# The end of a hybrid decoder step, cut into two halves of its tokens

## The chip, the cores and the metric

The kernel runs on one NeuronCore of a Trainium2 chip. Its time is the device time of one execution in microseconds (us); the kernel before has a median of 1413.08 us over three runs (1413.05 to 1415.09). The engines of the core work in parallel, each on its own list of instructions, and wait for each other through semaphores: TensorE (PE in the profile, with PEld for its weight loads) multiplies matrices, VectorE (DVE) and GpSimd (POOL) do elementwise work, ScalarE (ACT) does elementwise functions, and SyncE (SP) issues most transfers. ScalarE issues some transfers too.

## The reference

One decoder layer is applied to 264 tokens (256 of a prompt and 8 single tokens of a decoding batch), with a model width of 2048 and everything in float32:

```python
xn = rms_norm(x, g_mix)
z = xn @ w_in                       # five slices, for three mixers
# pooling branch, RG-LRU branch, Conformer branch -> y_pool, y_lru, y_conf
gates = sigmoid(xn @ w_gate + b_gate)
x = x + (g_a * y_pool + g_b * y_lru + g_c * y_conf) @ w_out
hid = square(relu(rms_norm(x, g_mlp) @ w_up))
x = x + hid @ w_down
y = x * rsqrt(mean(x * x, axis=-1) + 1e-6) * g_final
```

The last line is where the change lies. It can start for good only when the last column block of `hid @ w_down` has been added, since the mean goes over all 2048 features. The kernel also returns the new states of the three mixers.

## The kernel before

Activations are stored with features on the 128 partitions and tokens along the free dimension. `X` holds the 2048 features as 16 tiles (`KD`) of 128 x 264. Weights stream from memory in chunks of 128 x 1024 through SyncE; ScalarE rounds each chunk to a high part (`whi`, line 147), VectorE forms the low part (`wlo`, line 148), and three matmuls with the high and low parts (lines 151 to 153) stand for one float32 product. A loop over the chunks (line 847) gives out all instructions in one written order. After the last chunk of a group of four output tiles, an evacuation function is called for each of the four; work that may be done later is put in a list by `later(n, fn)` and given out by `run_bg`, at the end of the loop's round. Each engine takes its own instructions in the order in which they were given out.

For the last group (`w_down`, q = 3, tiles 12 to 15) the evacuation `down_evac` adds the result to `X` on VectorE (line 762) and puts off a function `rest`: it squares the tile on ScalarE (line 734), has GpSimd add the square to a running sum `sq2` (line 736; not for tiles 14 and 15, which keep their own squares), and scales the tile in place by `gfin`, which is -0.5 times `g_final` (line 767). The last two chunks are multiplied tile by tile, so tile 12 is complete first and tile 15 last.

Then comes the tail (lines 907 to 944). Three matmuls with a matrix of 1/2048 add the running sum and the two squares over the partitions and spread the mean to all of them (line 909). `root_seed` takes a logarithm and an exponential on ScalarE for a first inverse root (lines 209 and 210), and VectorE improves it by one Newton step in three instructions (lines 928, 929 and 931), which leave the factor in PSUM (`last`). ScalarE copies it to `rstd` in SBUF (line 932), which is what GpSimd reads. VectorE scales tiles 0 to 11 in place in six pieces of 1, 2, 3, 3, 2 and 1 tiles (line 936), each followed by a transfer on SyncE's queue (line 937); GpSimd scales tiles 12 to 15 one by one (line 940), each followed by a transfer on ScalarE's queue (line 941). The output in memory is laid out as partition, tile, token.

Between the root and the Newton step, 50 matmuls of ten shapes go to a PSUM buffer `probe` that nothing reads (lines 912 to 926). Two ScalarE instructions make operands for them: a copy of `whi` to bfloat16 (line 889), six chunks before the end, and a zeroed `wlo` chunk (line 911).

Of the kernel before, what the change touches and what calls it, by code (L numbers as in the profile page):

```python
# [9 lines left out]
F32 = mybir.dt.float32  # L10
F32R = mybir.dt.float32r
AF = mybir.ActivationFunctionType
ALU = mybir.AluOpType
AX = mybir.AxisListType

P = 128
D = 2048
# [28 lines left out]
NHI = 4  # L46
# [31 lines left out]
def hybrid_step(ctx: ExitStack, tc: tile.TileContext, x_in, par_in, st_in, wall, y_out, st_out):  # L78
# [5 lines left out]
    def f(ap):  # L84
        return ap.bitcast(F32)
# [24 lines left out]
    def acc():  # L110
        return psum.tile([P, 512], F32, name="acc", tag="acc")
# [58 lines left out]
    def mark(q, flag):  # L170
        stage(q, "none", 0.0, [lambda: done.add(flag)], 0)
# [34 lines left out]
    def root_seed(dst, ps, scale, load=True):  # L206
        if load:
            nc.scalar.preload_act_table_set(LN_EXP)
        nc.scalar.activation(dst, ps, AF.Ln, bias=eps, scale=scale)
        nc.scalar.activation(dst, dst, AF.Exp, scale=-0.5)  # L210
# [153 lines left out]
        stage("lru", "dve", 1.25, [lambda: gather(RA)])  # L364

    def lru_conv_sample():
        tmp = Gf[:, 8 * N:8 * N + 256].rearrange("p (c b k) -> p c b k", c=8, b=8)
        xs = XC[:, :, TP:N]

        def products():  # L370
            wb = pv("w_lru_conv").rearrange("p (c k) -> p c k", c=8)[:, :, None, :].to_broadcast([P, 8, 8, 4])
            nc.gpsimd.tensor_tensor(tmp, st_lc, wb, op=ALU.mult)
            nc.gpsimd.tensor_copy(st[:, O_LC:O_LC + 24].rearrange("p (c k) -> p c k", c=8), el[:, :, TP:TP + 3])

        def sums():
            nc.vector.tensor_reduce(xs, tmp, op=ALU.add, axis=AX.X)
            nc.vector.tensor_tensor(xs, xs, pv("b_lru_conv")[:, :, None].to_broadcast([P, 8, 8]), op=ALU.add)

        stage("lru", "pool", 1.0, [products])
        stage("lru", "dve", 0.5, [sums])  # L380

    def stage_split(q, n, hi, lo, x, gap=1):

        stage(q, "act", 0.65, [lambda i=i: nc.scalar.copy(hi(i), x(i)) for i in range(n)])
        stage(q, "dve", 0.71, [lambda i=i: nc.vector.tensor_tensor(lo(i), x(i), f(hi(i)), op=ALU.subtract)
                               for i in range(n)], gap)

    def lo_two(t, at=8):
        return lambda c: t[:, at + 2 * c:at + 2 * c + 2, :]

    def hi_two(t):
        return lambda c: t[:, 2 * c:2 * c + 2, :]
# [76 lines left out]
        stage("lru", "pool", 1.5, [sample])  # L469

    def gel_evac(ct, ps):
        nc.vector.tensor_tensor(GEL[:, ct, :], ps[:, :N], rstd, op=ALU.mult)
        spend(dve=0.4)

# [284 lines left out]
        later(2 + m % 4 // 2, other)  # L759

    def down_evac(q, m, ps):
        nc.vector.tensor_tensor(X[:, m, :], X[:, m, :], ps[:, :N], op=ALU.add)
        spend(dve=0.4)
        if q == 3:
            def rest():
                square_add(m, m < KD - 2)
                nc.scalar.activation(X[:, m, :], X[:, m, :], AF.Copy, scale=gfin[:, m:m + 1])

            later(0 if m >= KD - 4 else 1 + m % 4 // 2, rest)
# [28 lines left out]
    def after(gi):  # L798

        name, _, _, m = groups[gi]  # L800
        if name == "w_in":
            if m == 2:
                lru_conv(range(4, 8))
                lru_conv_sample()
                stage_split("lru", 4, hi_two(L), lo_two(L), lambda c: XC[:, 2 * c:2 * c + 2, :])
                mark("lru", "xc")
            elif m == 5:
                conf()
            elif m == 0:
                pooling()  # L810
            elif m in (3, 4):
                if m == 4:
                    gelu(0)
                    gelu(2)
                    stage_split("lru", 4, lambda c: LH(two(c)), lambda c: LH(slice(8 + 2 * c, 10 + 2 * c)),
                                lambda c: GEL[:, two(c), :])
                    mark("lru", "lru")
# [7 lines left out]
    def tile_mm(i, c, kt, m, rhs, pss, stop):  # L825
        s = slice(kt * 512 + m * P, kt * 512 + (m + 1) * P)
        xh, xl = rhs(2 * c + kt)
        mm3(pss[m], whi[:, i % NHI, s], wlo[:, i % NHI, s], xh, xl, c == 0 and kt == 0, stop)

    bw = Gf[:, :1024].bitcast(mybir.dt.bfloat16)  # L830
    zw = wlo[:, (len(chunks) - 3) % NHI, :]


    x_tile(0)
# [12 lines left out]
    for i, ch in enumerate(chunks):  # L847
        now[0] = i
        split(i + AHEAD)
        if i == 12:  # L850
            softplus()
            nc.vector.tensor_scalar(gfin, pv("g_final"), -0.5, None, op0=ALU.mult)
        if i % 2 == 0:
            dma_pair((i + 8) // 2)
        if i == 2:
            nc.sync.dma_start(par, par_in)
            nc.sync.dma_start(st[:, :S_IN], st_in)
        if i < 5:
            x_tile(2 * i + 6)
            x_tile(2 * i + 7)  # L860
        kind, gi, c, _ = ch
        if kind == "dense":
            rhs, fn = group(gi)
            n = groups[gi][2] // 2
            if c == 0:
                pss = [acc() for _ in range(4)]
            if i < len(chunks) - 2:
                if i == 0:
                    first_mm(rhs, pss)
                for kt in range(i == 0, 2):  # L870
                    for m in range(4):
                        tile_mm(i, c, kt, m, rhs, pss, c == n - 1 and kt == 1)
            elif i == len(chunks) - 1:
                for m in range(4):
                    for b in range(4):
                        tile_mm(i - 1 + b // 2, c - 1 + b // 2, b % 2, m, rhs, pss, b == 3)
            if c == n - 1:
                for m in range(4):
                    fn(m, pss[m])
                after(gi)  # L880
        elif kind == "lru":
            for j in range(2):
                lru_gate_mm(2 * gi + j, i, j)
            if gi == 3:
                lru_tail()
        elif kind == "grp":
            grp_mm(i)
        if i == len(chunks) - 6:
            nc.scalar.copy(bw, whi[:, 0:2, :].rearrange("p a n -> p (a n)"))
        if i == len(chunks) - 4:  # L890
            nc.scalar.preload_act_table_set(LN_EXP)
        if i == 140:
            nc.gpsimd.dma_start(st_out, st)
        if 5 <= i < 9:
            x_squares(i - 5)
        if i == 9:
            later(0, x_sum)
        if i == 11:
            later(0, x_rms)
        run_bg()  # L900
# [3 lines left out]
    assert not any(queues.values())  # L904


    ps = acc()
    for k, t in enumerate((20, 21 + (KD - 2) % 3, 21 + (KD - 1) % 3)):
        nc.tensor.matmul(ps[:, :N], ones, G[:, t, :], start=k == 0, stop=k == 2)  # L909
    root_seed(rstd, ps[:, :N], 1.0, False)  # L910
    nc.scalar.activation(zw, f(whi[:, 0, :]), AF.Copy, scale=0.0)
    probe = acc()
    flat = A.rearrange("p a n -> p (a n)")
    for n, p, m, at, what in ((512, P, P, 0, "b"), (N, P, P, 0, "b"), (512, P, P, 0, "r"), (512, P, P, 4, "r"),
                              (256, P, P, 0, "r"), (320, P, P, 0, "r"), (N, P, 64, 0, "r"), (N, 64, P, 0, "r"),
                              (N, P, P, 0, "f"), (N, P, P, 0, "z")):
        for j in range(5):
            if what == "b":
                w, v = bw[:, 1024 + j * P:1024 + (j + 1) * P], bw[:, :n]
            elif what == "r":  # L920
                w, v = whi[:p, j % 4, j * P:j * P + m], flat[:p, at:at + n]
            elif what == "z":
                w, v = zw[:, j * P:(j + 1) * P], zw[:, :n]
            else:
                w, v = f(whi[:, j % 4, j * P:(j + 1) * P]), f(flat[:, :n])
            nc.tensor.matmul(probe[:m, :n], w, v, start=True, stop=True)  # L926
    t = G[:, 9, :]
    nc.vector.tensor_tensor(t, rstd, rstd, op=ALU.mult)
    nc.vector.scalar_tensor_tensor(t, ps[:, :N], EPS, t, op0=ALU.add, op1=ALU.mult)
    last = acc()  # L930
    nc.vector.scalar_tensor_tensor(last[:, :N], t, -3.0, rstd, op0=ALU.add, op1=ALU.mult)
    nc.scalar.copy(rstd, last[:, :N])
    at, own = 0, KD - 4
    for n in (1, 2, 3, 3, 2, 1):
        s = slice(at, at + n)
        nc.vector.tensor_tensor(X[:, s, :], X[:, s, :], last[:, None, :N].to_broadcast([P, n, N]), op=ALU.mult)
        nc.sync.dma_start(y_out[:, s, :], X[:, s, :])
        if at and own < KD:
            s = slice(own, own + 1)
            nc.gpsimd.tensor_tensor(X[:, s, :], X[:, s, :], rstd[:, None, :], op=ALU.mult)  # L940
            nc.scalar.dma_start(y_out[:, s, :], X[:, s, :])
            own += 1
        at += n
    assert (at, own) == (KD - 4, KD)

# [84 lines left out]
```

## Time and profile before

| what | value |
|---|---|
| median of three runs | 1413.08 us (1413.05 to 1415.09) |
| the profiled execution: its own time, its span | 1414.92 us, 1413.1 us |
| TensorE busy | 1406.7 us, 100% |
| VectorE, ScalarE, GpSimd busy | 830.0, 721.8, 98.1 us |
| data moved | 256.95 MB, mean 182 GB/s |
| the tail, from the last evacuation to the end of the span | 1399.57 to 1413.1 us |

The span runs from the first to the last instruction of the profiled execution; the time of a run is taken around it and is a little longer. Times in rows are microseconds from the start of the span. In rows of the timeline the columns are start, duration, engine, line, operation, output and inputs with their shape, and a count; in brackets stand the idle time before it and what ended it. In rows of groups the two numbers after the first bar are the busy time in all and the mean of one instruction in nanoseconds. In rows of stretches the engines' busy times are followed by the granted share of TensorE's clock, the busy share of the transfer engines and the rate in GB/s.

### The profile page before, as it was taken

The numbers are of one execution on the slowest core, as the hardware profiler recorded it, in microseconds if no ns is written. First come the engines' busy times: TensorE is split into PE (matmuls) and PEld (weight loads), VectorE is DVE, ScalarE is ACT, GpSimd is POOL, SyncE is SP. The second block draws the span as 40 slices with busy tenths as digits, with TensorE's granted clock in tenths as the row PEclk, the third lists the DMA queues.
The fourth block names the chain that finished last, engine by engine and source line by source line (L and its number), as shares of the span: only waits on it lengthen the run. The fifth ranks groups of instructions, "written<-read, shape, count | busy, mean of one in ns | idle before, by whom it ended". The sixth has DMA issues, their size and how long they took to land.

```text
span 1413.1 us, 26699 instructions
## 1 busy us (share of the span) xinstructions
PE 1406.7 (100%) x11472; PEld 1402.5 (99%) x11473; DVE 830.0 (59%) x1031; ACT 721.8 (51%) x1007; POOL 98.1 (7%) x122
## 2 busy tenths in 40 slices
PE   9999999999999999999999999999999999999999
PEld 8999999999999999999999999999999999999998
DVE  6685787776766648665545444544455544455443
ACT  6657577656564645454544334543344533354544
POOL 0230010110102103010000000000000000000012
PEclk9999999999999999999999999999999999999999
DMA  9455455555655554555555555555555555555551
GB/s 331 150 184 195 167 195 193 179 179 180 209 179 179 179 179 150 209 179 179 180 179 180 182 179 180 182 180 183 181 183 183 183 181 183 180 179 179 179 179 62
DMA packets 38998, 256.95 MB, mean 182 GB/s; under 512 B 4320, under 2 KB 5472, under 8 KB 9440
## 3 DMA queue, kind: packets, MB, share of 16 engines
q1 hardware_dynamic: 38160, 253.67, 52.5%
q8 instruction: 89, 1.46, 0.4%
q0 software_dynamic: 144, 1.04, 0.2%
q10 hardware_dynamic: 576, 0.54, 0.1%
q14 instruction: 29, 0.24, 0.0%
HBM read 252.03 MB, written 3.21 MB: 181 GB/s over the span
## 4 chain that ended last, share of the span: by engine, by line
PE 98%; DMA 1%; POOL 0%; DVE 0%; SPq 0%; ACT 0%; issue 0%; ACTq 0%
PE acc L153 33%; PE acc L151 32%; PE acc L152 32%; PE acc L926 1%; DMA GX<-x_dram 1%; POOL tmp L689 0%; POOL G L541 0%; POOL G L540 0%; SPq L134 0%; DVE wlo L148 0%; PE acc L547 0%; ACT whi L147 0%; PE acc L222 0%; SPq L138 0%; PE acc L909 0%
## 5 line engine op out<-in xcount | busy, mean ns | idle before, releaser
L148 DVE TENSOR_TENSOR wlo<-raw,whi 128x1024 fp32r<-128x1024 f32 (+1 forms) x480 | 586.4, 1223 | 555.0 <-ACT whi L147 553.3
L147 ACT CAST whi<-raw 128x1024 fp32r<-128x1024 f32 (+1 forms) x480 | 497.6, 1038 | 631.8 <-PE acc L152 580.0
L151 PE MATMUL acc<-A,whi 128*128 128x264 f32 x1980 | 565.4, 286 | 1.6 <-ACT A L230 1.6
L153 PE MATMUL acc<-A,wlo 128*128 128x264 f32 x1980 | 564.1, 285 | 0.2 <-DVE wlo L148 0.2
L152 PE MATMUL acc<-A,whi 128*128 128x264 f32 x1980 | 563.3, 284 | 0.2
L151 PEld LDWEIGHTS acc<-A,whi 128*128 128x128 f32 x1980 | 374.0, 189 | 2.0 <-ACT A L230 1.8
L152 PEld LDWEIGHTS acc<-A,whi 128*128 128x128 f32 x1980 | 374.9, 189 | 0.7 <-DVE A L231 0.6
L153 PEld LDWEIGHTS acc<-A,wlo 128*128 128x128 f32 x1980 | 374.2, 189 | 0.4 <-DVE wlo L148 0.4
L151 PE MATMUL acc<-xn,whi 128*128 128x264 f32 x1024 | 291.9, 285 | 0.0
L153 PE MATMUL acc<-xn,wlo 128*128 128x264 f32 x1024 | 291.3, 284 | 0.0
L152 PE MATMUL acc<-xn,whi 128*128 128x264 f32 x1024 | 290.8, 284 | 0.0
L152 PEld LDWEIGHTS acc<-xn,whi 128*128 128x128 f32 x1024 | 193.5, 189 | 0.0
L153 PEld LDWEIGHTS acc<-xn,wlo 128*128 128x128 f32 x1024 | 193.1, 189 | 0.0
L151 PEld LDWEIGHTS acc<-xn,whi 128*128 128x128 f32 x1024 | 193.0, 189 | 0.0
L152 PE MATMUL acc<-Q,whi 128*128 128x264 f32 x644 | 182.6, 284 | 0.0
L153 PE MATMUL acc<-LH,wlo 128*128 128x264 f32 x640 | 182.3, 285 | 0.0
L151 PE MATMUL acc<-LH,whi 128*128 128x264 f32 x640 | 182.0, 284 | 0.0
L152 PEld LDWEIGHTS acc<-Q,whi 128*128 128x128 f32 x644 | 121.5, 189 | 0.0
L153 PEld LDWEIGHTS acc<-LH,wlo 128*128 128x128 f32 x640 | 120.4, 188 | 0.0
L151 PEld LDWEIGHTS acc<-LH,whi 128*128 128x128 f32 x640 | 120.4, 188 | 0.0
L736 POOL TENSOR_TENSOR G<-G 128x264 f32<-128x264 f32 x28 | 25.7, 917 | 809.9 <-ACT G L734 808.9
L522 ACT ACTIVATE G<-tmp,par 128x256 f32<-128x256 f32 x120 | 54.3, 500 | 1.3 <-DVE G L536 0.7
(179 smaller groups left out, 781.3 us busy)
## 6 DMA issues: line engine op xcount, KB each, us to landing
raw<-wall_dram SPq DMA_DIRECT2D x230, 1024.0 KB, 4.9
raw<-wall_dram SPq DMA_DIRECT2D x11, 512.0 KB, 7.7
GX<-x_dram SPq DMA_DIRECT2D x7, 264.0 KB, 8.1
raw<-wall_dram SPq DMA_DIRECT2D x7, 256.0 KB, 3.4
so_dram<-st POOLq DMA_DIRECT2D x1, 1018.0 KB, 6.1
st<-st_dram SPq DMA_DIRECT2D x1, 912.0 KB, 8.3
y_dram<-GX SPq DMA_DIRECT2D x2, 396.0 KB, 3.3
y_dram<-GX ACTq DMA_DIRECT2D x4, 132.0 KB, 2.6
```

The costliest lines, as they stand in the source:

```text
L147: nc.scalar.copy(h[:, s], r[:, s])
L148: nc.vector.tensor_tensor(lo[:, s], r[:, s], f(h[:, s]), op=ALU.subtract)
L151: nc.tensor.matmul(ps[:, :N], whi_t, xh, start=first, stop=False)
L152: nc.tensor.matmul(ps[:, :N], whi_t, xl, start=False, stop=False)
L153: nc.tensor.matmul(ps[:, :N], wlo_t, xh, start=False, stop=last)
L522: nc.scalar.activation(dst[:, ct, :TP], vext[:, ct, k:k + TP], AF.Copy, scale=par[:, w:w + 1])
L736: nc.gpsimd.tensor_tensor(sq2, sq2, t, op=ALU.add)
L926: nc.tensor.matmul(probe[:m, :n], w, v, start=True, stop=True)
```

## The change

The tail is written anew, by halves of 132 tokens:

- Tile 15 of the last group is added to `X` in two halves on VectorE, and each half is squared at once by ScalarE into `G[:, 11]`, in `down_evac` itself; its scaling by `gfin` is moved to the tail. Tiles 12, 13 and 14 keep the put-off `rest`.
- The sum over the partitions is taken for each half into its own PSUM buffer (six matmuls in place of three), and the logarithm and exponential for one half after the other.
- The first half's Newton step stays on VectorE. The second half's is made by four GpSimd instructions, from a copy of the mean plus epsilon that ScalarE makes; ScalarE then copies the factor to PSUM for VectorE.
- The scaled results go to two new buffers (in the space of `B0` and `B1`) in place of `X`. VectorE scales the first half in pieces of 2, 4, 5 and 5 tiles, then tiles 0 to 9 of the second half in pieces of 4, 4 and 2, with transfers on SyncE's queue; GpSimd scales tiles 10 to 15 of the second half in three pieces of 2, with transfers on ScalarE's queue.
- The output in memory is laid out as partition, half, tile, token, and put in order on the host by a transposition, as before.
- The 50 matmuls to `probe` and the two instructions that feed them are gone.
- The scratch of the short convolution's sample part moves from `G[:, 8]` to `CT` (`G[:, 12:16]`), with a mark that it is done.

```diff
     def lru_conv_sample():
-        tmp = Gf[:, 8 * N:8 * N + 256].rearrange("p (c b k) -> p c b k", c=8, b=8)
+        tmp = CT.rearrange("p c n -> p (c n)")[:, :256].rearrange("p (c b k) -> p c b k", c=8, b=8)
...
     def down_evac(q, m, ps):
+        if (q, m) == (3, KD - 1):
+            for s in (slice(0, N // 2), slice(N // 2, N)):
+                nc.vector.tensor_tensor(X[:, m, s], X[:, m, s], ps[:, s], op=ALU.add)
+                nc.scalar.activation(G[:, 11, s], X[:, m, s], AF.Square)
+            return
         nc.vector.tensor_tensor(X[:, m, :], X[:, m, :], ps[:, :N], op=ALU.add)
...
-        if i == len(chunks) - 6:
-            nc.scalar.copy(bw, whi[:, 0:2, :].rearrange("p a n -> p (a n)"))
...
-    ps = acc()
-    for k, t in enumerate((20, 21 + (KD - 2) % 3, 21 + (KD - 1) % 3)):
-        nc.tensor.matmul(ps[:, :N], ones, G[:, t, :], start=k == 0, stop=k == 2)
-    root_seed(rstd, ps[:, :N], 1.0, False)
-    nc.scalar.activation(zw, f(whi[:, 0, :]), AF.Copy, scale=0.0)
-    probe = acc()
...
-    nc.scalar.copy(rstd, last[:, :N])
-    at, own = 0, KD - 4
-    for n in (1, 2, 3, 3, 2, 1):
...
+    H2 = N // 2
+    half = [slice(0, H2), slice(H2, N)]
+    ps, last = [acc(), acc()], [acc(), acc()]
+    for k, t in enumerate((20, 21 + (KD - 2) % 3, 11)):
+        for h in range(2):
+            nc.tensor.matmul(ps[h][:, :H2], ones, G[:, t, half[h]], start=k == 0, stop=k == 2)
+    r = [rstd[:, half[h]] for h in range(2)]
+    for h in range(2):
+        root_seed(r[h], ps[h][:, :H2], 1.0, False)
+    out = [cpool.tile([P, KD, H2], F32, name=f"y{h}", tag=f"B{h}") for h in range(2)]
+    t, e = G[:, 9, :H2], G[:, 10, :H2]
+    nc.scalar.activation(e, ps[1][:, :H2], AF.Identity, bias=eps)
+    nc.scalar.activation(X[:, KD - 1, :], X[:, KD - 1, :], AF.Copy, scale=gfin[:, KD - 1:KD])
+    nc.vector.tensor_tensor(t, r[0], r[0], op=ALU.mult)
+    nc.vector.scalar_tensor_tensor(t, ps[0][:, :H2], EPS, t, op0=ALU.add, op1=ALU.mult)
+    nc.vector.scalar_tensor_tensor(last[0][:, :H2], t, -3.0, r[0], op0=ALU.add, op1=ALU.mult)
+    w = G[:, 12, :H2]
+    nc.gpsimd.tensor_tensor(w, r[1], r[1], op=ALU.mult)
+    nc.gpsimd.tensor_tensor(w, w, e, op=ALU.mult)
+    nc.gpsimd.tensor_scalar(w, w, 1.0, -3.0, op0=ALU.mult, op1=ALU.add)
+    nc.gpsimd.tensor_tensor(r[1], r[1], w, op=ALU.mult)
+    nc.scalar.copy(last[1][:, :H2], r[1])
+
+    def scaled(eng, h, a, n):
+        s = slice(a, a + n)
+        by = last[h][:, :H2] if eng is nc.vector else r[h]
+        eng.tensor_tensor(out[h][:, s, :], X[:, s, half[h]], by[:, None, :].to_broadcast([P, n, H2]), op=ALU.mult)
+        (nc.sync if eng is nc.vector else nc.scalar).dma_start(y_out[:, h, s, :], out[h][:, s, :])
+
+    for h, parts in ((0, (2, 4, 5, 5)), (1, (4, 4, 2))):
+        at = 0
+        for n in parts:
+            scaled(nc.vector, h, at, n)
+            at += n
+    for a in (10, 12, 14):
+        scaled(nc.gpsimd, 1, a, 2)
```

More of the change, by code (lines that the diff above doesn't have):

```diff
@@ L471, in gel_evac @@
     def gel_evac(ct, ps):
+        assert "conv" in done
         nc.vector.tensor_tensor(GEL[:, ct, :], ps[:, :N], rstd, op=ALU.mult)
@@ L804, in after @@
                 lru_conv_sample()
+                mark("lru", "conv")
                 stage_split("lru", 4, hi_two(L), lo_two(L), lambda c: XC[:, 2 * c:2 * c + 2, :])
@@ L828, in tile_mm @@
         mm3(pss[m], whi[:, i % NHI, s], wlo[:, i % NHI, s], xh, xl, c == 0 and kt == 0, stop)
-    bw = Gf[:, :1024].bitcast(mybir.dt.bfloat16)
-    zw = wlo[:, (len(chunks) - 3) % NHI, :]
     x_tile(0)
@@ L904, in hybrid_step @@
     assert not any(queues.values())
-    ps = acc()
-    for k, t in enumerate((20, 21 + (KD - 2) % 3, 21 + (KD - 1) % 3)):
-        nc.tensor.matmul(ps[:, :N], ones, G[:, t, :], start=k == 0, stop=k == 2)
-    root_seed(rstd, ps[:, :N], 1.0, False)
-    nc.scalar.activation(zw, f(whi[:, 0, :]), AF.Copy, scale=0.0)
-    probe = acc()
[L913 to L932, printed above, removed]
-    at, own = 0, KD - 4
-    for n in (1, 2, 3, 3, 2, 1):
[L935 to L943, printed above, removed]
@@ L944, in hybrid_step @@
-    assert (at, own) == (KD - 4, KD)
+    H2 = N // 2
[8 more added lines that the diff above has]
+    out = [cpool.tile([P, KD, H2], F32, name=f"y{h}", tag=f"B{h}") for h in range(2)]
@@ L1008 @@
             for n, v in arrays.items()]
-    args.append(nc.dram_tensor("y_dram", (P, KD, N), F32, kind="ExternalOutput").ap())
+    args.append(nc.dram_tensor("y_dram", (P, 2, KD, N // 2), F32, kind="ExternalOutput").ap())
     args.append(nc.dram_tensor("so_dram", (P, S_OUT), F32, kind="ExternalOutput").ap())
@@ L1014 @@
     y, so = r.results[0]["y_dram"], r.results[0]["so_dram"]
-    y = y.reshape(P, KD, N).transpose(2, 1, 0).reshape(N, D)
+    y = y.reshape(P, 2, KD, N // 2).transpose(1, 3, 2, 0).reshape(N, D)
     yp = np.ascontiguousarray(y[:TP])[None]
```

## The prediction

> **What bounds the kernel now.** I read the page's span and chain first, then the end of the chain in order of time, then what SyncE waits for last, then the engines one by one over the last 15 us.
>
> ```profile
> span 1413.1 us, 26699 instructions
> PE 98%; DMA 1%; POOL 0%; DVE 0%; SPq 0%; ACT 0%; issue 0%; ACTq 0%
> ...
> 1399.57 0.44 DVE GX L762
> ...
> 1400.09 0.43 ACT G L734
> ...
> 1400.57 0.71 PE acc L909 x2
> ...
> 1401.33 9.65 PE acc L926 x54
> ...
> SPq L1011 <- DMA y_dram<-GX: 2.4, 3, 1.3
> ...
> L1011 SPq DRAIN  x3: 7/7/7, 1412.3 to 1412.6; - x3
> ...
> 1411.00:1411.50 0.50, 0.00 (x0) 0.00 (x0) 0.00 (x0) 0.00 (x0) 0.00 (x0) 1.00 0.73 262
> ```
>
> TensorE is the bound for 1399.6 us, and the diff leaves that stretch alone. Only the last 13.5 us are in play. The chain view puts their larger part on the unused matmuls of L926. It is misleading there: those end at 1401.33 + 9.65 = 1410.98, output data moves until about 1411.4 (0.73 of the half microsecond from 1411.0), SyncE waits for output three times, and its drain follows at 1412.3. So the end is set by the output, and the output by when its first transfer can be issued:
>
> ```profile
> 1398.63 0.43 ACT L734 ACTIVATE G<-GX 128x264 f32<-128x264 f32 x1 [0.49 <-DVE GX L762]
> 1399.09 0.52 ACT L767 ACTIVATE GX<-GX,gfin 128x264 f32<-128x264 f32 x1
> 1400.09 0.42 ACT L734 ACTIVATE G<-GX 128x264 f32<-128x264 f32 x1 [0.48 <-DVE GX L762]
> 1400.55 0.51 ACT L767 ACTIVATE GX<-GX,gfin 128x264 f32<-128x264 f32 x1
> 1401.32 0.48 ACT L209 ACTIVATE rstd<-acc,eps 128x264 f32<-128x264 f32 x1 [0.26 <-PE acc L909]
> 1401.83 0.42 ACT L210 ACTIVATE rstd<-rstd 128x264 f32<-128x264 f32 x1
> 1402.16 1.04 ACT L911 ACTIVATE wlo<-whi 128x1024 fp32r<-128x1024 f32 x1
> 1403.75 0.38 ACT L932 COPY rstd<-acc 128x264 f32<-128x264 f32 x1 [0.55 <-DVE acc L931]
> ...
> 1402.29 0.43 DVE L928 TENSOR_TENSOR G<-rstd 128x264 f32<-128x264 f32 x1 [2.29 <-ACT rstd L210]
> ...
> 1404.16 3.77 DVE L936 TENSOR_TENSOR GX<-GX,acc 128x264 f32<-128x264 f32 x6 [0.50 <-ACT rstd L932]
> ...
> 1397.74 0.76 POOL L736 TENSOR_TENSOR G<-G 128x264 f32<-128x264 f32 x1 [0.70 <-ACT G L734]
> 1404.21 2.90 POOL L940 TENSOR_TENSOR GX<-GX,rstd 128x264 f32<-128x264 f32 x4 [5.72 <-ACT rstd L932]
> ...
> 1404.62 4.95 SPq L937 DMA_DIRECT2D y_dram<-GX  x6
> ```
>
> The tail reads: last matmul, last evacuation (1399.57), square of tile 15 (1400.09), its sum (1400.57), logarithm (1401.32), exponential, three VectorE steps, a copy that the first scaling waits for (0.50), scaling (1404.16), first transfer (1404.62). Tile 14 has been squared and scaled in the slack before 1399.61, and GpSimd added tile 13's square by 1398.50. Only tile 15's work lies behind the last matmul.
>
> **The change, step by step.** Durations of the narrower instructions come from these groups:
>
> ```profile
> L264 ACT ACTIVATE G<-GX 128x1056 f32<-128x1056 f32 x4 | 4.3, 1084 | 1.0 <-DVE G L268 1.0
> ...
> L936 DVE TENSOR_TENSOR GX<-GX,acc 128x792 f32<-128x792 f32 x2 | 1.9, 972 | 0.0
> L936 DVE TENSOR_TENSOR GX<-GX,acc 128x528 f32<-128x528 f32 x2 | 1.4, 696 | 0.0
> ...
> L302 POOL TENSOR_TENSOR G<-G 128x8 f32<-128x8 f32 x1 | 0.2, 206 | 0.1
> ...
> L926 PE MATMUL acc<-A,whi 128*128 128x264 f32 x10 | 2.5, 396 | 0.0
> ```
>
> ScalarE: 0.42 at 264 and 1.08 at 1056 is 0.84 ns an element, so a 132-wide form saves 0.11. VectorE: 0.69 and 0.97 at 528 and 792 is 1.04 ns, so 0.43 becomes 0.29. GpSimd: 0.21 at 8 and 0.76 at 264 gives 0.47. TensorE: a float32 pass of 264 columns is 0.25, so 0.12 for 132, and a float32 matmul is two passes.
>
> *Tile 15's square, moved.* Before, all four squares of the last group are put off to the background step; after, tile 15's two half squares are issued at its evacuation, while those of tiles 12, 13 and 14 are still put off. In the built program ScalarE's order is therefore: two half squares of tile 15, then square and scaling of 12, of 13, of 14, then the roots. ScalarE takes its instructions in order, so the three tiles, the last of them ready by 1398.63 today, now stand behind a wait for the last matmul. The halves of the evacuation end at 1399.86 and 1400.08 (0.29 each, the second overlapping a little), the half squares at 1400.45. A square and its scaling then take 0.46 + 0.42 = 0.88 (1400.09 to 1400.55, and an independent successor starts about 0.09 before its forerunner ends, as L911 does after L210): squares of 12, 13, 14 begin at 1400.36, 1401.24 and 1402.12. GpSimd's two additions (queued behind nothing else) are late next: the second waits for tile 13's square (1401.66), starts 0.13 later and takes 0.76, to 1402.55. The first of the sums waits for it.
>
> *Sums.* Six half matmuls replace three, and unlike before none can run ahead: the first needs that late addition. From 1402.60 the first half needs ten passes, 10 x 0.12 and about 0.2 of fill: first logarithm at 1404.05, against 1401.32. That is 2.73 late.
>
> *From logarithm to first transfer.* Before 1404.62 - 1401.32 = 3.30. Saved: 0.11 twice on ScalarE, 0.14 three times on VectorE, and the wait for the copy (0.50, of which 0.04 stays), 1.10 in all. The first piece is as large as before (264 elements). First transfer at 1404.05 + 2.20 = 1406.25, 1.63 late. One VectorE step (two operands in SBUF) may meet GpSimd's first root step; I take 0.15 for it, bounds 0 and 0.4.
>
> *Second root on GpSimd.* Four steps of 0.47 with gaps of 0.07 after the second exponential (first logarithm + 1.33) end at +3.5, the copy at +3.8. VectorE is busy with the first half until about +4.2 and the transfers with its data until about +6.3, so this costs nothing; that cover is about 1 us thick. GpSimd's own three scalings follow at +3.5 to +5.7, before VectorE's last at +5.9.
>
> *Output.* The same 2.16 MB in ten transfers:
>
> ```profile
> q1 hardware_dynamic: 864, 1.62, 36.7%
> q10 hardware_dynamic: 576, 0.54, 13.1%
> ...
> 1405.00:1406.00 1.00, 1.00 (x10) 0.96 (x9) 1.00 (x2) 0.00 (x0) 1.00 (x2) 1.00 0.48 165
> ```
>
> Over the 12 us from 1403 that is 49.8%, 5.98 us of all engines; data starts about 1405.5 (0.48 of that microsecond) and runs on to 1411.4, so it is bound by transfer. Rows get 1,056 to 2,640 bytes instead of 1,056 to 3,168: nothing, at most 0.1. The second piece is issued 0.61 after the first, and the first's 135 KB (0.37 us at 2.16 MB in 5.98 us) is gone by then: a gap of 0.24, where GpSimd's tile filled it before. Finishing after the last landing is unchanged.
>
> *Removed.* The 50 unused matmuls, with the ScalarE copies that feed two of them (L889, L911), were covered by output and by the stream: 0, bounds -0.3 (if L926 slowed the transfers) and 0. Scratch of the convolution moves to another place in G, no instruction changes its order there: 0.
>
> Sum with TensorE at its full clock: 1.63 + 0.15 + 0.24 + 0.05 = 2.1 us late.
>
> **The clock.** One term is left. TensorE now stands still from the last matmul (1399.5) to 1402.6, 3.1 us. The only such pause in this trace is at the start:
>
> ```profile
> 8.00:10.00 2.00, 1.20 (x10) 0.99 (x9) 0.27 (x1) 0.62 (x1) 0.00 (x0) 1.00 0.95 321
> 10.00:12.00 2.00, 1.05 (x4) 0.85 (x5) 1.61 (x4) 1.76 (x4) 0.00 (x0) 0.86 1.04 403
> 12.00:14.00 2.00, 2.00 (x11) 2.00 (x10) 2.00 (x5) 2.00 (x5) 0.00 (x0) 0.50 1.02 365
> 14.00:16.00 2.00, 2.00 (x15) 2.00 (x14) 1.75 (x4) 1.58 (x4) 0.00 (x0) 0.79 1.01 400
> ...
> 12.09 0.22 PE acc L151
> ...
> 1398.07 0.12 PE acc L151
> ```
>
> After a stretch in which TensorE was busy for about half of the time, the granted clock falls to 0.50 for some 3 us and a matmul's step goes from 0.12 to 0.22. A pause of 3.1 us should do the same, unless it ends before the clock is lowered. Ten passes at 0.23 instead of 0.12 are 1.1 us more: 3.2 in all. The moment of lowering is not set by the kernel, so the term lies between 0 and 1.1; I take 1.0, as the row's pause was shorter than ours.
>
> [...]
>
> Forecast: +3.1 us. The sum is made against the profiled span (1413.1, in an execution that took 1414.92); I add it to the median of the runs, 1413.08, as what lies around the span does not change: **1416.2 us**.
>
> **Rivals.**
> - *Full clock* in the late sums: +2.1, 1415.2. For it: 3.1 us may pass without the clock being lowered. Against it: the 0.50 row.
> - *Not slower: ScalarE's order costs nothing.* If tiles 12 to 14 were squared before 1399.6 as now, only tile 15's halves and one pair of sums would follow: first logarithm at about 1401.0, first transfer 1403.2, 1.4 early, less the gap and collision 0.4: 1412.1. It decides if the square of tile 12 starts before the last evacuation. Against it: every ScalarE row above starts in the program's order.
> - *Second root late.* If GpSimd's steps each wait for VectorE, the cover of 1 us is used up:
>
> ```profile
> L736 POOL TENSOR_TENSOR G<-G x28: 752/764/1409, 581.9 to 1397.7; 128x264 f32<-128x264 f32 x28
> ```
>
>   The longest is 0.65 over the shortest; four of those are 2.6, 1.6 beyond the cover: 1417.8. Against it: L940's four took 2.90 together beside L936, none stretched.
> - *The unused matmuls held the end.* If the finish waited for L926 (1410.98) and not for output, it would be early by the difference to its new cover, over 3 us: 1410. Against it: the drain at 1412.3.
>
> **How the numbers follow.** Half clock in all or most of the sums 0.52; full clock 0.33; second root late 0.07; ScalarE's order free 0.05; matmuls held the end 0.03. A measurement can tell about 0.2% (2.83 us, 1415.91) from no change. Half clock lies above that bound four times in five (0.42), late second root always (0.07), full clock hardly ever (0.03): slower 0.52. Faster by 0.2% (under 1410.25) is the last case: 0.03. Same: 0.45. The range leaves out the two earliest cases and the far side of the late root: 1414.0 to 1417.8. The likeliest case alone has 1415.4 to 1417.0.
>
> **What would show it.** ScalarE's first tail instruction is a half square of tile 15 at about 1399.9, tile 14's square at about 1402.1; GpSimd's last addition ends near 1402.55; the first logarithm starts at 1404.05 (full clock) or 1405.1 (half), first transfer 2.2 to 2.4 later, the last data about 7.1 after that; PEclk near 0.5 at 1403 to 1405. The prediction is wrong if the first logarithm starts before 1403, if output has gaps beyond 0.3 us, or if the transfer's 6 us change.

## The result, and the profile after

Before, the median of 21 runs was 1413.35 us (1412.82 to 1415.66); after, the median of 21 runs taken in turn with them was 1416.4 us (1414.62 to 1417.43). The ratio is 1.0017 with a 95% interval of 1.0011 to 1.0022: slower by 2.4 us (1.6 to 3.1). The times of both kernels gather at two values about 2 us apart, before 15 runs up to 1414.02 and 6 from 1414.49, after 10 runs up to 1415.77 and 11 from 1416.4, so that the two medians (3.05 apart) compare a lower value with an upper one; like with like, the medians of the lower runs are 2.0 apart (1413.14 and 1415.13) and those of the upper ones 2.2 (1414.89 and 1417.09).

The profiled execution of after took 1417.07 us, that of before 1414.92. First, from the page of after, the span and the chain's shares:

```profile
span 1415.3 us, 26610 instructions
...
PE 98%; POOL 1%; DVE 1%; DMA 0%; ACT 0%; issue 0%; SPq 0%; DVEq 0%; POOLq 0%
```

GpSimd now has 1% of the chain, where the page of before had 0%. The end of that chain in order of time (start, us, engine, output, line):

```profile
1399.40 0.30 DVE GX L765
...
1399.73 0.52 ACT G L766 x2
1400.24 0.32 ACT G L735
...
1400.70 0.74 POOL G L737
...
1401.56 0.75 POOL G L737
...
1402.35 1.93 PE acc L914 x10
...
1404.31 0.38 ACT rstd L209
...
1405.71 0.56 DVE acc L924
...
1406.30 1.80 DVE y L935 x3
```

Between the half squares of tile 15 (L766) and its sum (L914) stand a square of another tile (L735) and two GpSimd additions (L737), 2 us of work that before was done ahead of the last matmul. The timeline shows the queues behind it (in brackets the idle time before, and what ended it):

```profile
1399.73 0.52 ACT L766 ACTIVATE G<-GX 128x132 f32<-128x132 f32 x2 [9.80 <-DVE GX L765]
1400.15 0.41 ACT L735 ACTIVATE G<-GX 128x264 f32<-128x264 f32 x1
...
1401.87 0.41 ACT L735 ACTIVATE G<-GX 128x264 f32<-128x264 f32 x1
1404.31 0.37 ACT L209 ACTIVATE rstd<-acc,eps 128x132 f32<-128x132 f32 x1 [1.48 <-PE acc L914]
...
1400.70 1.60 POOL L737 TENSOR_TENSOR G<-G 128x264 f32<-128x264 f32 x2 [18.16 <-ACT G L735]
...
1406.76 5.25 SPq L936 DMA_DIRECT2D y_dram<-y  x7
...
1402.35 2.36 PE L914 MATMUL acc<-G,ones 128*128 128x132 f32 x12 [2.99 <-POOL G L737]
```

ScalarE stood idle for 9.80 us in front of tile 15's half squares, with the squares of tiles 12 to 14 queued behind them; GpSimd had been idle for 18.16 us when the first of those released its two additions. TensorE had paused for 2.99 us when the last addition let its sums begin. The stretches (PE, weight loads, DVE, ACT and POOL busy, then the granted clock, the transfers' share and GB/s):

```profile
1401.00:1403.00 2.00, 0.65 (x5) 0.65 (x6) 0.00 (x0) 1.76 (x5) 1.18 (x2) 1.00 0.00 0
1403.00:1405.00 2.00, 1.71 (x9) 1.40 (x7) 0.00 (x0) 0.66 (x3) 0.00 (x0) 0.52 0.00 0
...
1413.00:1414.00 1.00, 0.00 (x0) 0.00 (x0) 0.00 (x0) 0.00 (x0) 0.00 (x0) 0.50 0.61 226
```

The clock was still full when the sums began and fell to a half at 1403.07 (0.52 as a mean over two microseconds), in their midst: the first of the twelve passes of the sums begin 0.11 us apart, the last ones 0.22. Output data runs on to 1413.6 (0.61 of the last stretch).

The two executions did not reach the tail at the same moment (last evacuation at 1399.57 before and 1399.40 after), although their code is the same up to there. From here on every time in the tail is therefore counted from the start of the kernel's own last evacuation, and the "tail" is from there to the span's end:

| kernel | median of runs (number), us | last evacuation | first logarithm | first transfer | tail |
|---|---|---|---|---|---|
| before | 1413.35 (21) | 1399.57 | +1.75 | +5.05 | 13.58 |
| after | 1416.4 (21) | 1399.40 | +4.91 | +7.36 | 15.90 |
| e1_square_last | 1411.8 (11) | 1397.74 | +1.23 | +3.68 | 12.21 |
| e2_pe_busy | 1415.06 (11) | 1398.35 | +4.39 | +6.84 | 15.39 |
| e3_order_alone | 1416.89 (8) | 1397.78 | +5.13 | +8.43 | 16.97 |
| e4_no_unused | 1413.04 (11) | 1397.83 | +1.75 | +5.05 | 13.43 |
| e5_two_mends | 1411.54 (11) | 1397.62 | +1.22 | +3.43 | 11.94 |
| e6_late_root | 1412.53 (1) | 1398.08 | +1.22 | +3.68 | 12.69 |
| e7_long_pause | 1419.77 (1) | 1397.50 | +9.54 | +12.00 | 20.52 |

e1 to e4 shared 30 runs of before (median 1413.37), e5 to e7 another 15 (1413.31). After's tail is 2.32 longer than before's, close to the ratio's 2.4.

### The profile page after: what moved, and what is told of

Its sections match the earlier page's. It is cut to its first block, busy times and chain, and to the rows that moved or that the text cites. A ratio compares the mean times of both kernels' runs of the same rounds, so it can differ in the third digit from the quotient of the medians.

```text
span 1415.3 us, 26610 instructions
## 1 busy us (share of the span) xinstructions
PE 1398.6 (99%) x11424; PEld 1396.5 (99%) x11424; DVE 830.7 (59%) x1033; ACT 719.0 (51%) x1009; POOL 98.9 (7%) x125
## 4 chain that ended last, share of the span: by engine, by line
PE 98%; POOL 1%; DVE 1%; DMA 0%; ACT 0%; issue 0%; SPq 0%; DVEq 0%; POOLq 0%
PE acc L153 33%; PE acc L151 32%; PE acc L152 32%; DMA GX<-x_dram 0%; POOL tmp L690 0%; DVE y L935 0%; PE acc L914 0%; DVE wlo L148 0%; POOL G L542 0%; POOL G L737 0%; POOL G L541 0%; PE acc L548 0%; ACT whi L147 0%; PE acc L222 0%; SPq L134 0%
## 5 line engine op out<-in xcount | busy, mean ns | idle before, releaser
L737 POOL TENSOR_TENSOR G<-G 128x264 f32<-128x264 f32 x28 | 25.6, 916 | 813.9 <-ACT G L735 812.8
```

What stands on the lines that cost most here:

```text
L737: nc.gpsimd.tensor_tensor(sq2, sq2, t, op=ALU.add)
```

## The experiments

The theory: ScalarE's order is the cause, and the half clock adds to it. The rival: the work by halves is itself dearer, with twice the instructions, GpSimd's root and more pieces of output. The extra matmuls of e2 and the extra GpSimd instructions of e6 and e7 make results that nothing uses; e4 leaves out only matmuls whose results nothing used.

**e1_square_last: the halves kept, the order mended.** Tile 15's half squares join the put-off steps behind tiles 12 to 14. Against after:

```diff
-                nc.scalar.activation(G[:, 11, s], X[:, m, s], AF.Square)
+                later(0, lambda s=s: nc.scalar.activation(G[:, 11, s], X[:, m, s], AF.Square))
```

> The changed kernel with one edit: tile 15's half squares are put off like the other tiles' work, so that ScalarE squares tiles 12, 13 and 14 first. If ScalarE's order is the cause, the three tiles are done before the last evacuation, only one pair of half sums is left behind it, TensorE pauses for under 1 us and keeps its clock: first logarithm about 1.2 us after the last evacuation begins (before: 1.75, changed kernel: 4.91), first transfer about 3.7 after it (before 5.05), end of the span about 1.1 earlier than before: 1412.2 us. Rival, the halves themselves cost the time (a second root on GpSimd, more and smaller instructions and transfers): the end stays within 1 us of the changed kernel's, 1415.4 or more.

Measured: 1411.8 us (1411.45 to 1413.29), ratio to before 0.999 (0.9981 to 0.9999), a gain of 1.4 us (0.1 to 2.7). The timeline of e1:

```profile
1396.81 0.43 ACT L735 ACTIVATE G<-GX 128x264 f32<-128x264 f32 x1 [0.49 <-DVE GX L768]
...
1398.07 0.52 ACT L766 ACTIVATE G<-GX 128x132 f32<-128x132 f32 x2 [0.29 <-DVE GX L765]
1398.97 0.37 ACT L209 ACTIVATE rstd<-acc,eps 128x132 f32<-128x132 f32 x1 [0.38 <-PE acc L914]
...
1397.74 0.49 DVE L765 TENSOR_TENSOR GX<-GX,acc 128x132 f32<-128x132 f32 x2 [1.03 <-PE acc L153]
...
1400.37 0.55 DVE L924 SCALAR_TENSOR_TENSOR acc<-G,rstd 128x132 f32<-128x132 f32 x1
...
1400.36 0.41 POOL L926 TENSOR_TENSOR G<-rstd 128x132 f32<-128x132 f32 x1 [3.70 <-ACT rstd L210]
...
1401.42 5.23 SPq L936 DMA_DIRECT2D y_dram<-y  x7
```

Tile 14's square is at 1396.81, ahead of the last evacuation, and the half squares wait 0.29 for that evacuation only. The logarithm comes at +1.23 instead of +4.91. The order costs 15.90 - 12.21 = 3.69 us of after's tail (a part of it through the clock, as e2 shows), and the rest of the change gains 13.58 - 12.21 = 1.37. The rival falls: by halves the tail is shorter.

**e2_pe_busy: the order kept, TensorE kept busy.** 22 extra matmuls fill the pause ahead of the sums. Against after:

```diff
+    probe = acc()
+    for j in range(22):
+        nc.tensor.matmul(probe[:, :N], whi[:, 0, :P], A[:, 0, :], start=True, stop=True)
```

> The changed kernel with 22 matmuls of 264 columns to a PSUM buffer that nothing reads, ahead of the sums, so that TensorE works through most of its pause (22 x 0.12 = 2.6 us of 3.0). If the half clock is a term of its own, the granted clock stays at 1.00 from 1403 to 1405, twelve passes of the sums keep a step of 0.11, the first logarithm comes 0.3 us earlier than in the profiled execution of the changed kernel (where the clock fell in the middle of the sums), and the median lies 0.3 to 1.1 below that of the changed kernel: about 1415.6. Rival, the clock follows something else than TensorE's pause: 0.50 is seen again and the time stays at 1416.4.

Measured: 1415.06 us (1414.7 to 1417.08), ratio 1.0012 (1.0003 to 1.0021). The timeline and the stretches of e2:

```profile
1398.15 2.82 PE L914 MATMUL acc<-A,whi 128*128 128x264 f32 x22
1401.31 1.62 PE L917 MATMUL acc<-G,ones 128*128 128x132 f32 x12 [0.34 <-POOL G L737]
...
1402.74 0.37 ACT L209 ACTIVATE rstd<-acc,eps 128x132 f32<-128x132 f32 x1 [0.96 <-PE acc L917]
```

```profile
1401.00:1403.00 2.00, 1.62 (x12) 1.42 (x12) 0.00 (x0) 1.01 (x3) 0.26 (x1) 1.00 0.00 0
```

At a clock of 1.00 the twelve passes take 1.62 instead of 2.36, and from the first of them to the logarithm it is 1.43 (1401.31 to 1402.74) instead of 1.96 (1402.35 to 1404.31). The clock cost the profiled execution of after 0.53, and its tail 0.51 (15.90 against 15.39). By far the larger part of the loss is there at full clock too: against e1, whose sums also ran at full clock (1.00 up to 1402), the order costs 15.39 - 12.21 = 3.18. The median lies 1.34 below after's, more than the 0.3 to 1.1 that was expected, but only 0.07 below that of after's lower runs (1415.13).

**e3_order_alone: the order on the old tail.** Before, with tile 15 squared whole at its evacuation, and nothing by halves. Against before:

```diff
+        if m == KD - 1:
+            nc.scalar.activation(G[:, 11, :], X[:, m, :], AF.Square)
...
-        square_add(m, m < KD - 2)
+        if m < KD - 1: square_add(m, m < KD - 2)
...
-    for k, t in enumerate((20, 21 + (KD - 2) % 3, 21 + (KD - 1) % 3)):
+    for k, t in enumerate((20, 21 + (KD - 2) % 3, 11)):
```

> The kernel before with one edit: tile 15's square, whole, is issued in its evacuation and so stands ahead of the work of tiles 12, 13 and 14 on ScalarE. No halves, same roots, same output, same unused matmuls. If the order is the cause, tile 13's square ends about 2.1 us after the last evacuation begins, GpSimd's last addition 3.0 after, the first logarithm 4.7 after (before 1.75) at full clock and up to 5.8 at half clock, and everything behind it moves along: 2.9 to 4.0 slower than before, about 1416.7. Rival, the order is absorbed and the halves cost the time: within 0.5 us of before.

Measured: 1416.89 us (1415.87 to 1419.51), ratio 1.0026 (1.0016 to 1.0036). The timeline of e3:

```profile
1398.24 0.42 ACT L766 ACTIVATE G<-GX 128x264 f32<-128x264 f32 x1 [9.94 <-DVE GX L762]
1398.57 0.41 ACT L734 ACTIVATE G<-GX 128x264 f32<-128x264 f32 x1
...
1402.91 0.48 ACT L209 ACTIVATE rstd<-acc,eps 128x264 f32<-128x264 f32 x1 [1.25 <-PE acc L913]
...
1399.12 1.60 POOL L736 TENSOR_TENSOR G<-G 128x264 f32<-128x264 f32 x2 [18.20 <-ACT G L734]
```

```profile
1401.00:1403.00 2.00, 2.00 (x7) 1.29 (x7) 0.00 (x0) 0.74 (x3) 0.00 (x0) 0.69 0.00 0
```

The same picture as after's: 9.94 us of idle ScalarE ahead of tile 15, GpSimd's additions after 18.20 us of idle time, the logarithm at +5.13. One instruction moved ahead of others in its queue lengthens the old tail by 16.97 - 13.58 = 3.39 us. The clock has a share in this number too: it fell at 1401.76, in the midst of these sums (the 0.69). Their passes begin 0.22 us apart before that and 0.44 after it, and the last takes 0.65 instead of 0.39, which makes about 0.5 us by estimate. So the order alone costs about 2.9 us at full clock, and the logarithm would stand at about +4.6, where 4.7 was expected.

**e4_no_unused: the unused matmuls away.** Before, without the 50 matmuls to `probe` and the two ScalarE instructions that feed them:

```diff
-            nc.scalar.copy(bw, whi[:, 0:2, :].rearrange("p a n -> p (a n)"))
...
-    nc.scalar.activation(zw, f(whi[:, 0, :]), AF.Copy, scale=0.0)
-    probe = acc()
```

> The kernel before without the 50 unused matmuls and the two ScalarE instructions that make their operands. If the output ends the kernel, nothing changes: first transfer, last data and end of the span within 0.2 us, median within 0.5 us of before. Rival, the unused matmuls held the end, or slowed the transfers: 0.5 to 3 us faster, 1410.4 to 1412.9.

Measured: 1413.04 us (1412.54 to 1415.05), ratio 0.9998 (0.9989 to 1.0007). The timeline of e4:

```profile
1399.58 0.48 ACT L209 ACTIVATE rstd<-acc,eps 128x264 f32<-128x264 f32 x1 [0.26 <-PE acc L907]
...
1402.88 4.91 SPq L919 DMA_DIRECT2D y_dram<-GX  x6
```

Logarithm and first transfer stand at +1.75 and +5.05, as before. The line that took most of the tail in the chain's summary of before held nothing up; the tail differs by 0.15, which these runs can't tell from nothing.

**e5_two_mends: two smaller mends.** On e1, the first step of GpSimd's root goes to ScalarE, so that VectorE's third step meets no GpSimd instruction, and VectorE's first pieces are smaller. Against e1:

```diff
+    w = G[:, 12, :H2]
+    nc.scalar.activation(w, r[1], AF.Square)
...
-    nc.gpsimd.tensor_tensor(w, r[1], r[1], op=ALU.mult)
...
-    for h, parts in ((0, (2, 4, 5, 5)), (1, (4, 4, 2))):
+    for h, parts in ((0, (2, 2, 4, 4, 4)), (1, (4, 4, 2))):
```

> The kernel of e1_square_last with two more edits: the first half goes out in pieces of 2, 2, 4, 4 and 4 tiles instead of 2, 4, 5 and 5 (the second transfer is issued 0.35 after the first instead of 0.61), and the square of the second root is made by ScalarE instead of GpSimd. If the gap after the first piece and the meeting of VectorE's third step with GpSimd's first are the two small terms of the sum, that step takes 0.31 instead of 0.55, transfers run without a gap, and the tail (from the last evacuation to the end of the span, 12.25 in e1_square_last) is 11.8. Rival, both are hidden by the transfer: 12.2 or more. The median can't tell 0.4 us; it should lie at 1411.4, 1412.0 at most.

Measured: 1411.54 us (1411.19 to 1412.08), ratio 0.9986 (0.9977 to 0.9995): a gain of 2.0 us on before (0.7 to 3.3). The timeline of e5:

```profile
1400.25 0.30 DVE L926 SCALAR_TENSOR_TENSOR acc<-G,rstd 128x132 f32<-128x132 f32 x1
...
1401.05 4.91 SPq L936 DMA_DIRECT2D y_dram<-y  x8
```

The VectorE step took 0.55 beside a GpSimd step that began with it (e1's rows at 1400.36 and 1400.37), and 0.30 without one. The first transfer moved by the same 0.25 and the tail by 0.27 (to 11.94, where 11.8 was expected), so that the smaller pieces added nothing to speak of: in place of one short stretch with less data behind the first piece the transfers now have two (shares of 0.64 and 0.67 in the quarters of a microsecond from 1402.25 and 1402.75).

**e6_late_root: the second root late.** On e1, four extra GpSimd instructions ahead of the root of the second half:

```diff
+    for _ in range(4):
+        nc.gpsimd.tensor_tensor(G[:, 13, :H2], r[1], r[1], op=ALU.mult)
```

> The kernel of e1_square_last with four more GpSimd steps of 132 columns, whose result nothing reads, ahead of the second root: 4 x (0.46 + 0.07) = 2.1 us later. If the cover of the second root is about 1 us thick, the tail grows by 0.8 (0.5 to 1.2) from 12.25 to 13.05, with VectorE waiting about 1.2 us between the halves. Rival, no cover: 2.1 more, 14.35. Rival, cover thicker than 2 us: 12.25.

Measured: one execution of 1412.53 us; tail 12.69, 0.48 more than e1's, just under the lower edge of what was expected. The timeline of e6:

```profile
1400.70 1.86 POOL L927 TENSOR_TENSOR G<-rstd 128x132 f32<-128x132 f32 x4 [3.69 <-ACT rstd L210]
...
1404.74 1.66 DVE L937 TENSOR_TENSOR y<-GX,acc 128x528 f32<-128x528 f32 x3 [0.89 <-ACT acc L932]
```

The four take 1.86; VectorE waits 0.89 of that between its halves, and only 0.48 reaches the end. About 1.0 us of a late root is hidden by VectorE's first half, and 0.4 more by transfers that are still under way: their share stays at 1.03 up to 1405.5 and then falls to 0.33 and 0.70 for half a microsecond each, 0.49 us in all without data.

**e7_long_pause: the pause made long.** On after, six extra GpSimd instructions between tiles 12 and 13, to see what the clock can cost at most:

```diff
+        if m == 12 and last:
+            for _ in range(6):
+                nc.gpsimd.tensor_tensor(G[:, 13, :], t, t, op=ALU.mult)
```

> The changed kernel with six more GpSimd additions' worth of work (264 columns, result unread) ahead of its last two additions, which lengthens TensorE's pause from 3.0 to about 7.4 us. If the clock falls in every pause that is long enough, it is at 0.50 before the sums begin, all twelve passes take a step of 0.22, and from the end of GpSimd's last addition to the first logarithm it is 2.6 us (2.0 in the profiled execution of the changed kernel, 1.5 in e2_pe_busy): 1.1 is the upper end of the clock's term. Rival, a step of 0.11 in any pass: the term has another cause. The tail is 5 us longer than the changed kernel's 15.9.

Measured: one execution of 1419.77 us; tail 20.52. The timeline and the stretches of e7:

```profile
1404.44 3.00 PE L917 MATMUL acc<-G,ones 128*128 128x132 f32 x12 [6.98 <-POOL G L740]
...
1407.04 0.37 ACT L209 ACTIVATE rstd<-acc,eps 128x132 f32<-128x132 f32 x1 [6.12 <-PE acc L917]
```

```profile
1399.00:1401.00 2.00, 0.00 (x0) 0.00 (x0) 0.00 (x0) 1.85 (x5) 1.76 (x4) 0.65 0.00 0
...
1405.00:1407.00 2.00, 2.00 (x11) 2.00 (x10) 0.00 (x0) 0.00 (x0) 0.00 (x0) 0.50 0.00 0
```

After a pause of 6.98 us all the sums run at half clock, and from the first pass to the logarithm it takes 2.60. With e2's 1.43 and after's 1.96 that is a series: the clock's term is 0 in e2, 0.53 in the profiled execution of after, and 1.17 at its largest.

## Why the prediction was right, and where its sizes were off

The time, the range and the mechanism held; the likeliest case's term for the clock did not hold as forecast.

- **The output sets the end, and the unused matmuls cost nothing: right.** e4 took them away alone and neither the first transfer nor the time moved.
- **Tile 15 ahead of tiles 12 to 14: right, and the whole cause.** Tile 14's square began at 1401.87 (forecast 1402.12, with the evacuation 0.17 earlier), GpSimd's additions ended at 1402.30 (forecast 1402.55). At full clock (e2) the logarithm came at +4.39; the forecast was 4.48. e1 and e3 show the order from both sides: undone, it gives back 3.69, alone, it costs 3.39, and in each about 0.5 is the clock.
- **Logarithm to first transfer, forecast 2.20 and 0.15 for VectorE meeting GpSimd: right within 0.1.** It was 2.45 (1404.31 to 1406.76), 0.1 over the two together. The meeting cost 0.25 (0.55 against 0.30 in e5).
- **The second root at no cost under a cover of 1 us: right.** e6 held GpSimd for 1.86 ahead of the root: VectorE waited for 0.89 of it, so its cover was about 1.0, and the end moved by no more than 0.48. The rival in which the root comes late had counted what passes the cover in full.
- **Output, forecast 0.24 for a gap and 0.05 for the rows: too large.** From the first transfer's issue to the last data it is 6.8 us before (1404.62 to 1411.4) and 6.8 after (1406.76 to 1413.6); to 0.1 us there is no cost. The gap itself is there (a share of 0.28 in the quarter of a microsecond from 1408.0, about 0.2 us without data); why the end did not move with it is not shown.
- **The clock, taken as 1.0 between bounds of 0 and 1.1: the term that was mis-sized.** In the profiled execution it was 0.53, because the clock fell in the middle of the sums; the bounds nearly held, with e2 at 0 and e7 at 1.17. The forecast took it that a pause longer than the row's would lower the clock ahead of the sums. In after it fell 3.7 us after the pause had begun (1402.35 - 2.99 = 1399.36 to 1403.07), 0.72 us into the sums; in e7 2.1 us after (1404.44 - 6.98 = 1397.46 to 1399.60, the 0.65 of 1399 to 1401), 4.84 us ahead of them. What sets the moment is not shown. That the kernel does not set it, as the forecast has it, agrees with the start, where the kernels do the same work and the clock fell to a half in two of the nine profiled executions (the last section).

Sum by sum, the profiled execution's tail grew by 2.32 where 3.1 was forecast: 0.5 too much for the clock and 0.3 too much for the output, while the logarithm (0.1 early) and the way to the first transfer (0.1 long) cancel. That the median of after came out 0.2 from the forecast is therefore partly owed to where the median falls between the two gatherings of its times; like with like, the loss is 2.0 to 2.2 us, which is nearer to the rival with a full clock (+2.1). e2, with its clock held, has a median of 1415.06, and after's lower runs one of 1415.13. That speaks for a full clock, or nearly, in those of after's runs, and so do their mean clocks: four of the ten have 0.997 or 0.998, which, if half clock is all that lowers the mean, puts the fall at most about 10 us before the end (2 x 0.0035 x 1413 = 9.9, where 0.0035 is the most that 0.997 can stand for), behind the logarithm (11 us before the end in after and e2). The other six have 0.996, where it can't be told, and only one execution of after was profiled. How often the clock falls during the sums, and why more of after's runs (11 of 21) than of before's (6 of 21) lie at the upper value, stays open. By estimate, a run with all sums at half clock and none at the start would take about 1416.2 (e2's 1415.06 and e7's 1.17), so that some of the eleven may be of that kind.

## What to carry to other kernels

ScalarE took its instructions in order in every row shown above, so issuing a step "at once" can make it later work's gate: put the last tile's step behind everything that is already able to run, and look in the timeline for a long idle time in front of it with ready work queued behind. Shortening a chain pays only if the order ahead of it is kept: here the shorter chain was worth 1.4 us and the order cost 3.4 to 3.7 (2.9 to 3.2 at full clock), so with that one line mended and a meeting of two engines avoided (e5) the same change makes 1411.54 us, faster than both kernels. And measure a tail from the last event of the part that is unchanged, since the time to reach that event varied by 2.1 us here, almost as much as the change.

## What the runs showed of the hardware

The moment of the last evacuation, in code that is the same up to it, was 1399.57 and 1399.40 in the profiled executions of before and after, and 1397.50 to 1398.35 in the seven others. The difference is at the start. Stretches of after, and then of e1:

```profile
10.00:12.00 2.00, 2.00 (x11) 1.70 (x10) 1.54 (x3) 1.77 (x5) 0.00 (x0) 0.61 1.00 362
12.00:14.00 2.00, 2.00 (x11) 2.00 (x11) 2.00 (x5) 2.00 (x6) 0.00 (x0) 0.54 1.02 387
```

```profile
10.00:12.00 2.00, 1.39 (x9) 1.19 (x10) 1.75 (x5) 1.90 (x5) 0.00 (x0) 1.00 1.03 379
12.00:14.00 2.00, 2.00 (x19) 2.00 (x18) 2.00 (x5) 2.00 (x4) 0.00 (x0) 1.00 1.01 378
```

In the first two the clock was at about a half from 10 to 14 us, as in the rows of before; from 12 to 14 us eleven matmuls ran where e1, at full clock, ran nineteen. In all seven experiments the clock stayed at 1.00 there. The two executions with the lower clock (1414.92 and 1417.07 us) belong to the upper gatherings of their kernels, and each run has a mean granted clock beside its time: of the 30 runs of before beside e1 to e4, the 22 up to 1413.65 us have 1.000 and the eight from 1414.41 us 0.998 or 0.999. One thousandth of 1413 us is 1.4 us of lost clock, most of the distance. Where in those runs it was lost, only a profile would show. In after the lower ten have 0.996 to 0.998 and the upper eleven 0.994 to 0.996, a mixture that includes the idle output at the end.

A second thing is when the clock changed. At the start it fell at 11.43 us in before and at 10.44 in after, and in both it was full again 3.41 us later (rows of narrow stretches show it): 3.41 us at half clock or 1.7 us lost; their last evacuation came 1.1 to 2.1 us later than in the others. TensorE was at work ahead of both falls, for 1.20 us (before) and 1.22 (after) of the two from 8 to 10; in the seven experiments, where the clock stayed full, it was busy for 1.27 to 2.00 of them.

In the tail the same six sums lost 0, 0.53 and 1.17 us in e2, after and e7, behind pauses of 0.34, 2.99 and 6.98 us. From the start of the pause to the fall it was 3.7 us in after, 2.1 in e7 and, by estimate, 4.0 in e3 (TensorE was busy for 7.74 of the ten microseconds from 1390, taken as up to 1397.74, and the clock fell at 1401.76). By these three a pause of 3 us ends before the fall, as it did in after and e3, or, at e7's 2.1, behind it; what sets this time is not shown.
